# A hybrid decoder step on one core: half of down's token sums made in down, one accumulator bank for four products of the up quarters, operands asked for ahead, norms spread, the end by blocks

## The chip, the cores and the metric

The kernel runs on one core of one Trainium2 chip. The metric is the device time of one execution in microseconds. A core has five engines that run their own instruction streams beside each other: TensorE (PE: matrix products, with its weight loads shown as PEld), VectorE (DVE), ScalarE (ACT), GpSimd (POOL) and SyncE (SP, which here only issues DMAs). Products accumulate in eight PSUM banks; operands lie in SBUF; DMAs move data between SBUF and device memory.

## The reference, cut to what matters

One decoder layer for 2048 prompt tokens and 64 sample tokens (8 sequences of 8), width 1024: a mixer (DeltaNet heads and windowed attention), an output projection, then a gated ConvFFN with 2 x 2816 hidden columns, and a last RMSNorm. The change lies almost wholly in the FFN and the last norm:

```python
h = _rmsnorm(x, norm_ffn_w[i]) * (1 + sc2) + sh2
u = jnp.einsum('bld,df->blf', h, ffn_w_up[i])               # up
u_c, n_f_buf = _causal_dwconv(u, f_buf, ffn_conv_w[i])      # width 3
gate, up = jnp.split(u_c + ffn_conv_b[i], 2, axis=-1)
x = x + g2 * jnp.einsum('blf,fd->bld', jax.nn.silu(gate) * up, ffn_w_down[i])   # down
...
y = _rmsnorm(x, final_norm_w)
```

## The kernel before, in words

**Layout.** Tokens run along the free dimension, channels along the 128 partitions. Every fp32 product is made of three passes: each operand is split into a high part (rounded, `...h`) and a low part (the rest, `...l`), and PE forms high x high, low x high and high x low. So each operand that comes from memory costs an ACT cast (the high part) and a DVE or POOL subtraction (the low part).

**Stages.** adaLN and the input projection (0 to about 760 us of the span), mixer, output projection, `up_proj` for the first half of the tokens and a few channel blocks of the second, then the *up quarters* (about 1830 to 2280), then *down* (to the end).

**Beside the first stages** `weight_sums` (L1547) makes sums of down's weight blocks (`ws_d`): it loads two blocks into `suv` (L1553), takes four DVE sums (L1556 to L1559) and stores them (L1562). Its loads stand in SP's queue among those of the adaLN weights (`wada`) and the input projection (`w_raw`). The adaLN result is copied by ACT (`ms`, L184) and transposed by PE (`adat_ps`, L188).

**The up quarters** (`up_quarters`, `Quarters`) form, for the second half of the tokens (1088 of them: 384 + 384 + 320), two channel blocks per step p (a gate block and an up block) by the seven-product scheme for 2 x 2 blocks (products of sums). The weights of step p come in two 512-KB loads, `rawu` and `rawg`; POOL makes the sums S1, S2 (L1353, L1354) and S3, S4 (L1356, L1357); each of the eight operands of a step is then split by ACT (`rh`, L1360) and DVE or POOL (`rl`, L1361) into a ring of six. `prods` (L1426) says which operand goes into which bank: `a`, `b`, `c` for the 384-token products, `u` and `g` for the 320-token ones. After each product `evac` (L1450) brings a bank out: before the change bank `a` is copied to `t1` by ACT (L1455), bank `b` is added to `t1` by DVE (L1457, L1462, L1466), each time before `b` is used again. `elementwise` (L1471) then does the convolution (ACT: Identity, L1437; DVE: taps, L1435), the gate (ACT Tanh, L1479; DVE, L1481) and the product with the up half (L1488), whose result `actq` is stored to `act_d`.

**Token sums.** down uses the seven-product scheme too, with the hidden channels in two halves, K1 and K2, of 11 blocks, and the tokens in two halves. So it needs, beside the plain blocks B.., four sums over tokens: T1 to T4. Before the change all four are made in the quarters: `diff_loads` (L1387) reads the first half's results back, into `d12` and `d22`, and `diffs` (L1397) makes, for each p of K1, three DVE subtractions (T3, T1, T2) with a store each, and for each p of K2 one or two (T4). SP issues all this in order: a load into `d12` or `d22` waits until the store from that buffer has landed, and the next weight load stands behind it.

**down** (`down_phase`, L1577) runs over two parts of the tokens (`ip`), and in each over the seven entries of `DOWN` (L1568: weight operand, token operand, token group, whether new accumulators start, where the result goes). An entry has 11 steps i; each loads a weight tile (`wr`, 128 x 512) and a token tile (`tr`, 128 x 512 or 576), splits both (L1599 ACT, L1600 DVE; six buffers of each), and issues 24 matmuls (`products`, L1641). The last three steps are done accumulator by accumulator, so that the residual (`residual`, L1184) and the sums of squares for the last norm can start. The norm (`norm`, L1604) takes the sums over channels on PE (`ss_ps`), the root on DVE and POOL, brings it to all partitions by PE (`rb_ps`) and ACT (`drB`), and multiplies: four tiles on DVE (L1617), four on POOL (L1615). It is a generator; it is advanced between the products of the next entry, which starts with only six of its eight accumulators while a norm is pending (`free`). At the very end the last 576 tokens are done as blocks of 320 and 256 in the order of the last three steps only; both norms come after the last products.

**What sets the order.** Each engine runs its instructions in the order in which this code issues them, sorted by the tile framework; waits come from buffers and banks that are used again.

Of the kernel before, what the change touches and what calls it, by code (L numbers as in the profile page):

```python
# [94 lines left out]
def kernel(  # L95
# [22 lines left out]
    ts_d = {t: scratch(f"{t}_d", [KH, P, n]) for t, n in (("T1", LH), ("T2", LT - LH), ("T3", LH), ("T4", LT - LH))}  # L118
# [233 lines left out]
    def rest(steps):  # L352
        for _ in steps:
            pass
# [854 lines left out]
    def up_proj(hf, h, uc, op, ms=range(MU)):  # L1209
# [3 lines left out]
        def evac(m, bi, ps):  # L1213
# [7 lines left out]
            if m % 2 == 0:  # L1221
                silu2(cv, rb)
            else:
                nc.vector.tensor_tensor(cv, cv, sg[bi], ALU.mult)
                nc.sync.dma_start(act_d[m // 2, :, c0:c0 + n], cv)
# [146 lines left out]
    def up_quarters(first, q, h, W, uc, us, pq, sums_done):  # L1372
# [14 lines left out]
        def diff_loads(p):  # L1387
            if p in K1:
                for t, k in ((d12, p), (d22, K2[K1.index(p)])):
                    nc.sync.dma_start(t[:, :LH], act_d[k, :, :LH])  # L1390
                return
            i = K2.index(p)
            nc.sync.dma_start(d22, ts_d["T2"][i])
            if i + 8 < KH:
                nc.sync.dma_start(d12, ts_d["T2"][i + 8])

        def diffs(p):  # L1397
            sub = lambda out, a, b: nc.vector.tensor_tensor(out, a, b, ALU.subtract)
            if p in K1:
                i = K1.index(p)  # L1400
                sub(sg[:, :LH], d22[:, :LH], d12[:, :LH])
# [11 lines left out]
            if i + 8 < KH:  # L1413
                nc.sync.dma_start(sg, act_d[K2[i + 8], :, c0:])
            sub(d22, act, d22)
            nc.sync.dma_start(ts_d["T4"][i], d22)
            yield
            yield
            if i + 8 < KH:
                sub(d12, sg, d12)  # L1420
                nc.sync.dma_start(ts_d["T4"][i + 8], d12)
# [4 lines left out]
        prods = [[("B11", "a"), ("X1", "u")], [("T2", "b")], [("B21", "a"), ("X2", "u")], [("T3", "b")], [("X1", "g")],  # L1426
# [23 lines left out]
        def evac(j, bk, ru, rg):  # L1450
# [3 lines left out]
            if j == 0:  # L1454
                copy(t1, ps("a"))  # L1455
            elif j == 1:
                tt(U2, ps("b"), t1, ALU.add)  # L1457
            elif j == 2:
                copy(ru[:, cols[0]], ps("a"))
                copy(ru[:, cols[2]], bk["u"][:, :n - 2 * nx])  # L1460
            elif j == 3:
# [536 lines left out]
```

## Time and profile before

| | us |
|---|---|
| median of 3 runs | 2795.57 (2795.16 to 2802.66) |
| profiled execution, whole | 2792.84 |
| its span | 2791.1 |
| outside its span | 1.74 |

The profile's busy shares of the span are 95% for PE, 69% for DVE, 46% for ACT and 29% for POOL; the mean granted clock of TensorE is 0.979 of full.

By stage, of the same profiled execution:

| stage, us of the span | PE busy | DVE | ACT | POOL | clock | GB/s |
|---|---|---|---|---|---|---|
| 0 to 760 | 707.80 | 541.72 | 355.47 | 241.34 | 0.98 | 159 |
| quarters, 1830 to 2254 | 404.75 | 338.74 | 188.22 | 236.93 | 0.98 | 166 |
| end of the quarters, down, 2254 to 2791 | 497.60 | 323.19 | 227.20 | 70.04 | 0.96 | 192 |

In the views of the trace a group's row has line, engine, operation, output <- inputs (buffer numbers left out), shape, count, then busy time, mean duration in ns, and the idle time of the engine just before with what ended it. A waits row has engine, tile, line, what it waited for, then total us, times, longest. A windows row has the stretch, its length, busy time and count of PE, PEld, DVE, ACT and POOL, the granted clock, the busy share of the DMA engines and GB/s. A timeline row has start, duration and instruction, in brackets the idle time before it and its releaser.

### The profile page before, as it was taken

The numbers are of one execution on the slowest core, as the hardware profiler recorded it, in microseconds if no ns is written. First come the engines' busy times: TensorE is split into PE (matmuls) and PEld (weight loads), VectorE is DVE, ScalarE is ACT, GpSimd is POOL, SyncE is SP. The second block draws the span as 40 slices with busy tenths as digits, with TensorE's granted clock in tenths as the row PEclk, the third lists the DMA queues.
The fourth block names the chain that finished last, engine by engine and source line by source line (L and its number), as shares of the span: only waits on it lengthen the run. The fifth ranks groups of instructions, "written<-read, shape, count | busy, mean of one in ns | idle before, by whom it ended". The sixth has DMA issues, their size and how long they took to land.

```text
span 2791.1 us, 52033 instructions
## 1 busy us (share of the span) xinstructions
PE 2651.8 (95%) x19394; PEld 2480.7 (89%) x19394; DVE 1923.3 (69%) x3947; ACT 1270.9 (46%) x3327; POOL 822.6 (29%) x711
## 2 busy tenths in 40 slices
PE   7899999999999899999999999899999989999997
PEld 6788987788999898888888999899989989999997
DVE  6666479898413887888777646888877765665655
ACT  5444265554322654554544534554334444443443
POOL 2015243442313422222131114246555600121021
PEclk9999999999999999999999999999999999999998
DMA  7874443332445443332264445134455557565644
GB/s 278 297 269 143 127 135 108 90 98 78 133 122 187 141 118 87 96 95 74 72 215 134 142 144 190 64 118 169 156 182 187 171 177 246 178 205 193 223 154 138
DMA packets 311177, 428.21 MB, mean 153 GB/s; under 512 B 82275, under 2 KB 217924, under 8 KB 310660
## 3 DMA queue, kind: packets, MB, share of 16 engines
q1 hardware_dynamic: 310924, 424.89, 47.0%
q8 instruction: 152, 2.49, 0.4%
q14 instruction: 101, 0.83, 0.1%
HBM read 304.71 MB, written 121.09 MB: 153 GB/s over the span
## 4 chain that ended last, share of the span: by engine, by line
PE 69%; DVE 15%; DMA 6%; ACT 3%; issue 3%; POOL 2%; SPq 1%; DVEq 0%; ACTq 0%; POOLq 0%
PE up_ps L323 18%; PE dn_ps L1641 15%; PE in_ps L323 12%; PE op_ps L323 6%; DVE ev L522 2%; PE uq_b L1510 2%; DMA T_d<-d 2%; DMA rawg<-in_w_upT_dram 1%; PE uq_c L1510 1%; PE as_ps L917 1%; PE pv_ps L954 1%; PE uq_a L1510 1%; PE uq_g L1510 1%; PE uq_u L1510 1%; DVE gt L699 1%
## 5 line engine op out<-in xcount | busy, mean ns | idle before, releaser
L323 PE MATMUL up_ps<-hi,w_hi 128*128 128x384 f32 (+2 forms) x1152 | 379.5, 329 | 8.7 <-ACT cv L517 7.9
L323 PE MATMUL up_ps<-hi,w_lo 128*128 128x384 f32 (+2 forms) x1152 | 373.9, 325 | 1.0 <-DVE w_lo L315 1.0
L323 PE MATMUL up_ps<-lo,w_hi 128*128 128x384 f32 (+2 forms) x1152 | 371.6, 323 | 0.0
L1641 PE MATMUL dn_ps<-tl,wh 128*128 128x256 f32 (+1 forms) x1232 | 354.5, 290 | 14.2 <-DVE tl L1600 14.2
L1641 PE MATMUL dn_ps<-th,wl 128*128 128x256 f32 (+1 forms) x1232 | 353.3, 290 | 0.0
L323 PE MATMUL in_ps<-hi,w_hi 128*128 128x384 f32 (+2 forms) x1056 | 347.1, 333 | 6.2 <-DVE ev L572 2.6
L323 PE MATMUL in_ps<-lo,w_hi 128*128 128x384 f32 (+2 forms) x1056 | 348.5, 330 | 2.2 <-DVE lo L265 1.3
L323 PE MATMUL in_ps<-hi,w_lo 128*128 128x384 f32 (+2 forms) x1056 | 346.2, 328 | 0.5 <-POOL w_lo L315 0.5
L1641 PE MATMUL dn_ps<-th,wh 128*128 128x256 f32 (+1 forms) x1232 | 337.2, 289 | 8.5 <-DVE actq L1488 7.6
L1641 PEld LDWEIGHTS dn_ps<-tl,wh 128*128 128x128 f32 x1232 | 239.6, 194 | 15.3 <-DVE tl L1600 15.3
L323 PEld LDWEIGHTS up_ps<-hi,w_hi 128*128 128x128 f32 x1152 | 219.2, 190 | 30.5 <-issue 15.9
L1641 PEld LDWEIGHTS dn_ps<-th,wl 128*128 128x128 f32 x1232 | 239.3, 194 | 0.0
L1641 PEld LDWEIGHTS dn_ps<-th,wh 128*128 128x128 f32 x1232 | 230.2, 192 | 9.3 <-issue 7.8
L323 PEld LDWEIGHTS up_ps<-hi,w_lo 128*128 128x128 f32 x1152 | 218.8, 190 | 9.3 <-issue 7.0
L323 PEld LDWEIGHTS up_ps<-lo,w_hi 128*128 128x128 f32 x1152 | 219.0, 190 | 7.1 <-issue 6.2
L323 PEld LDWEIGHTS in_ps<-hi,w_hi 128*128 128x128 f32 x1056 | 200.1, 191 | 19.6 <-issue 10.3
L323 PEld LDWEIGHTS in_ps<-lo,w_hi 128*128 128x128 f32 x1056 | 201.3, 191 | 14.9 <-issue 9.5
L323 PEld LDWEIGHTS in_ps<-hi,w_lo 128*128 128x128 f32 x1056 | 201.4, 191 | 5.9 <-issue 4.4
L314 ACT CAST w_hi<-w_raw 128x1024 fp32r<-128x1024 f32 x124 | 129.6, 1046 | 120.8 <-PE op_ps L323 48.4
L1600 DVE TENSOR_TENSOR wl<-wr,wh 128x512 fp32r<-128x512 f32 x154 | 110.6, 718 | 106.7 <-ACT wh L1599 106.6
L315 DVE TENSOR_TENSOR w_lo<-w_raw,w_hi 128x1024 fp32r<-128x1024 f32 x95 | 119.1, 1254 | 91.5 <-ACT w_hi L314 89.1
L522 DVE SCALAR_TENSOR_TENSOR ev<-rb,cw,ev 128x384 f32<-128x384 f32 (+1 forms) x216 | 149.8, 698 | 42.8 <-ACT ev L515 40.5
(478 smaller groups left out, 6664.0 us busy)
## 6 DMA issues: line engine op xcount, KB each, us to landing
w_raw<-in_w_upT_dram SPq DMA_DIRECT2D x50, 512.0 KB
wada<-in_w_ada_dram SPq DMA_DIRECT2D x44, 512.0 KB
w_raw<-in_w_inT_dram SPq DMA_DIRECT2D x44, 512.0 KB
wr<-ws_d SPq DMA_DIRECT2D x88, 256.0 KB
proj<-ev SPq DMA_DIRECT2D x88, 192.0 KB
wr<-in_w_downT_dram SPq DMA_DIRECT2D x66, 256.0 KB
tr<-T_d SPq DMA_DIRECT2D x66, 256.0 KB
w_raw<-in_w_outT_dram SPq DMA_DIRECT2D x32, 512.0 KB
```

Source lines behind the costliest of these rows:

```text
L314: nc.scalar.copy(hi, raw)
L315: (eng or nc.vector).tensor_tensor(lo, raw, hi.bitcast(F32), ALU.subtract)
L323: nc.tensor.matmul(ps[:, :n], a[:, k, :], b[:, k, :n], start=first is not False and k == ks[0] and i == 0, stop=last is not False and k == ...
L522: nc.vector.scalar_tensor_tensor(out, src(j), w[:, j:j + 1], out, ALU.mult, ALU.add)
L699: nc.vector.tensor_tensor(tv, G[:np_, j, j + 1:].unsqueeze(2).broadcast_to(shape), T0[:, j, 0:j + 1].unsqueeze(1).broadcast_to(shape), ALU ...
L917: nc.tensor.matmul(banks[v][:, 256 * g + P * k0:256 * g + 256], qs[r, g0 + g], kw[r, P * k0:], start=True, stop=True, tile_position=(64 * ...
L954: nc.tensor.matmul(pv_ps[64 * v:64 * v + 64, :], (vprev[0], vt)[half][:, 64 * v:64 * v + 64], PT[v, half], start=half == k0, stop=half == 1)
L1510: nc.tensor.matmul(bk[t][:, :nb], u[:, k], v[:, k], start=new and k == 0 and y == 0, stop=k == KG - 1 and y == 2, skip_group_check=True)
L1600: nc.vector.tensor_tensor(l, raw, h.bitcast(F32), ALU.subtract)
L1641: nc.tensor.matmul(acc[m, s][:, :width[s]], w[i][a][:, c], t[i][b][:, r], start=new and i == 0 and y == 0, stop=i == KH - 1 and y == 2, sk ...
```

## The change

1. **Early loads.** `weight_sums` asks for its two blocks only behind the last weight load that was issued (`tc.issue_after(loads[-1])`).
2. **Silu.** `up_proj` for the second half of the tokens and the quarters use ACT's Silu in place of Tanh and a DVE instruction; the factor 2 that the rest of the code carries goes into the multiplication with the up half (a TENSOR_TENSOR becomes a SCALAR_TENSOR_TENSOR).
3. **One bank for four products.** In the quarters B11, T2, T3 and T4 of the up scheme now add up in bank `b` without a restart; ACT copies the running sum out after each (`t1`, U2, U3, then the gate block). The three DVE adds onto `t1` are gone; a DVE add for B21 (bank `a` plus `t1`) takes the place of an ACT copy.
4. **Token sums.** In the quarters a K1 step makes only T3 and T1 (T1 now 1088 tokens wide, one store), a K2 step only E, the difference of its own two halves. T2 = B22 - T1 and T4 = T1 + E are made in down, from two loads (`tr` and a new `tx`, two buffers) and one DVE instruction per step.
5. **Operands ahead.** down asks for the operands of step i + 3 ahead of the products of step i, across entries too (`ahead`, `AHEAD` = 3).
6. **Norms spread.** The norm's parts are advanced behind the first steps (i = 1 and 3) of the next entry's first pass, not after it.
7. **The end by blocks.** The last entry runs all 11 steps for its block of 320 tokens, then all 11 for the block of 256; the weights of steps 6 to 10 stay in buffers of their own, the first block's norm runs beside the second block's products, and the last sum of squares is kept apart (`dsl`).
8. **Banks at down's start.** The list of banks is permuted for the first entry (`banks[:1] + banks[4:] + banks[1:4]`).

```diff
-        prods = [[("B11", "a"), ("X1", "u")], [("T2", "b")], [("B21", "a"), ("X2", "u")], [("T3", "b")], [("X1", "g")],
+        prods = [[("B11", "b"), ("X1", "u")], [("T2", "b")], [("B21", "a"), ("X2", "u")], [("T3", "b")], [("X1", "g")],
                  [("T1", "c")], [("T4", "b"), ("X2", "g")], [("B22", "c")]]
...
-            if j == 0:
-                copy(t1, ps("a"))
-            elif j == 1:
-                tt(U2, ps("b"), t1, ALU.add)
+            if j in (0, 1, 3):
+                copy((t1, U2, None, U3)[j], ps("b"))
             elif j == 2:
-                copy(ru[:, cols[0]], ps("a"))
+                tt(ru[:, cols[0]], ps("a"), t1, ALU.add)
...
-            nc.scalar.activation(rg[:, :n], dg, AF.Tanh, scale=0.5)
+            nc.scalar.activation(sg, dg, AF.Silu)
             yield
-            nc.vector.scalar_tensor_tensor(sg, rg[:, :n], 1.0, dg, ALU.add, ALU.mult)
...
-                sub(d12[:, :LH], d12[:, :LH], act[:, :LH])
-                nc.sync.dma_start(ts_d["T1"][i], d12[:, :LH])
                 yield
-                sub(d22[:, :LH], d22[:, :LH], d12[:, :LH])
-                nc.scalar.copy(d22[:, LH:], act[:, LH:])
-                nc.sync.dma_start(ts_d["T2"][i], d22)
+                sub(d12, d12, act)
+                nc.scalar.mul(d12[:, LH:], act[:, LH:], -1.0)
+                nc.sync.dma_start(ts_d["T1"][i], d12)
...
             for x, k in enumerate((K1[i], K2[i])):
-                nc.sync.dma_start(uv[:, x], I["w_downT"][k])
+                with tc.issue_after(loads[-1]):
+                    nc.sync.dma_start(uv[:, x], I["w_downT"][k])
...
+            if name == "T2":
+                raw, more = get("tr", "T1", r, RAWS), get("tx", "B22", slice(r.start, min(r.stop, PW)), 2)
+                c = more.shape[1]
+                nc.vector.tensor_tensor(raw[:, :c], more, raw[:, :c], ALU.subtract)
...
+            elif name == "T4":
+                raw, more = get("tr", "T1", r, RAWS), get("tx", "E", r, 2)
+                nc.vector.tensor_tensor(raw, raw, more, ALU.add)
...
+                for i in range(lead):
+                    ahead(f + min(i + AHEAD, DR - 1))
+                    products(i, head)
+                    if finish and i in (1, 3):
+                        next(finish)
...
+            if last:
+                for s in (1, 0):
+                    f = place[q, 0, subs[s].start]
+                    for i in range(KH - SIDE):
+                        ahead(f + i + AHEAD)
+                        products(i, [(m, s) for m in range(NM)])
+                        if finish and i:
+                            next(finish, None)
```

**How the rows move.** In SP's queue in the early stage, before the change, the first `suv` loads of the weight sums stand ahead of the projection's stores and loads:

```order
L479 DMA tu_s<-zero 64x512 [waits DMAHW5_49]
L1553 DMA suv<-in_w_downT_dram 128x1024 [waits DMAHW6_49]
L1553 DMA suv<-in_w_downT_dram 128x1024 [waits DMAHW7_49]
L578 DMA proj<-ev 128x384 [waits DMAHW0_49,DVE_49]
L306 DMA w_raw<-in_w_inT_dram 128x1024 [waits DMAHW1_49,Pool_49]
```

After the change, in SP's queue, they stand here:

```order
L168 DMA wada<-in_w_ada_dram 128x1024 [waits DMAHW7_49,PE_49]
L578 DMA proj<-ev 128x384 [waits DVE_49]
L306 DMA w_raw<-in_w_inT_dram 128x1024 [waits Pool_49]
L1547 DMA suv<-in_w_downT_dram 128x1024 [waits DMAHW2_49]
L1547 DMA suv<-in_w_downT_dram 128x1024 [waits DMAHW3_49]
L578 DMA proj<-ev 128x256 [waits DMAHW4_49,DVE_49]
```

They moved from the queue's positions 45 and 46 to 97 and 98, that is behind 52 other DMAs, and their DVE sums with them.

On ACT, inside one K1 step of the quarters, before the change (`rh` the casts of operands, `t` the copy of bank a, `rbg` the gate block, S the weight sums that POOL makes):

```order
L1360 CAST rh<-S_20422 128x512 [waits PE_49]
L1455 COPY t_21095<-uq_a 128x384 [waits PE_49]
L1360 CAST rh<-rawg 128x512 [waits PE_49]
L1479 ACTIVATE rbg_21092<-cq 128x1088 [waits DVE_49,Activation_49]
L1360 CAST rh<-S_21099 128x512 [waits PE_49,Pool_49]
L1459 COPY rbu_21090<-uq_a 128x384 [waits PE_49]
L1437 ACTIVATE cq<-rbu_21091,vcb,vcw 128x1088 [waits DVE_49]
```

After the change ACT has these rows at the same place of a step, up to the fourth copy of bank b (t, U, U, rbg):

```order
L1453 COPY t_21085<-uq_b 128x384 [waits PE_49]
L1363 CAST rh<-rawu 128x512 [waits DVE_49,PE_49]
...
L1473 ACTIVATE sgq<-cq 128x1088 [waits DMAHW4_49,DVE_49,Activation_49]
L1435 ACTIVATE cq<-rbu_21080,vcb,vcw 128x1088 [waits Activation_49]
L1363 CAST rh<-S_21089 128x512 [waits PE_49,Pool_49]
L1453 COPY U_21086<-uq_b 128x384 [waits PE_49]
...
L1363 CAST rh<-S_20421 128x512 [waits PE_49,Pool_49]
L1453 COPY U_21087<-uq_b 128x384 [waits PE_49]
...
L1460 COPY rbg_21082<-uq_b 128x384 [waits PE_49]
```

Bank b is now copied out four times per step by ACT, each copy behind a cast or an activation; two of the casts ahead of them wait for POOL.

On PE, where down's first norm falls between the products of the next entry, before the change (buffer numbers kept; `ss_ps` the sums of squares, `rb_ps` the root brought to all partitions, the last row the first product whose operand DVE makes behind the norm's multiplications):

```order
L214 MATMUL ss_ps_27245<-ones_82,dsum2_26565 128x1 [waits Pool_49]
...
L1641 MATMUL dn_ps_27084<-tl_27306,wh_27299 128x256 [waits DVE_49]
...
L222 MATMUL rb_ps_27259<-dg_27254,ones_82 128x128 [waits DVE_49]
L1641 MATMUL dn_ps_27265<-th_27098,wh_27092 128x256 [waits PE_49]
...
L222 MATMUL rb_ps_27259<-dg_27254,ones_82 128x128 [waits DVE_49] x3
L1641 MATMUL dn_ps_27266<-th_27098,wh_27092 128x256 [waits Activation_49]
...
L1641 MATMUL dn_ps_27084<-tl_27345,wh_27338 128x256 [waits DVE_49]
```

After the change PE has this there:

```order
L214 MATMUL ss_ps_27181<-ones_81,dsum2_26591 128x1 [waits DVE_49,Pool_49]
...
L1690 MATMUL dn_ps_27110<-tl_27125,wh_27118 128x256 [waits DVE_49]
...
L1690 MATMUL dn_ps_27110<-tl_27155,wh_27148 128x256 [waits DVE_49]
...
L222 MATMUL rb_ps_27243<-dg_27190,ones_81 128x128 [waits DVE_49] x4
...
L1690 MATMUL dn_ps_27267<-th_26978,wh_26972 128x256 [waits PE_49]
...
L1690 MATMUL dn_ps_27110<-tl_27308,wh_27301 128x256 [waits DVE_49]
```

Between the last `rb_ps` row and that product stand 28 matmuls before the change and 66 after it. DVE's own order there is the same in both: root, four `dg`, four multiplications, then the low parts of the next step.

At down's start the accumulators of both programs take the banks in one order (0, 7, 6, 5, 4, then 3, 2, 1): the permuted list does not show in the program as it is built.

More of the change, by code (lines that the diff above doesn't have):

```diff
@@ L1465, in evac @@
             elif j == 6:
-                tt(rg[:, cols[0]], ps("b"), t1, ALU.add)
+                copy(rg[:, cols[0]], ps("b"))
                 copy(rg[:, cols[2]], bk["g"][:, :n - 2 * nx])
@@ new lines, in down_phase, with ahead @@
+        blocks_of = lambda q, g: [slice(0, SW), slice(SW, wide(q, g))]
+        queue = [(q, i, slice(0, wide(q, DOWN[q % ND][2]))) for q in range(Q - 1) for i in range(KH)]
+        queue += [(Q - 1, i, blocks_of(Q - 1, 1)[s]) for s in (1, 0) for i in range(KH)]
+        place = {(q, i, r.start): f for f, (q, i, r) in enumerate(queue)}
+        done = [0]
+        def ahead(f):
+            while done[0] <= min(f, len(queue) - 1):
+                q, i, r = queue[done[0]]
+                get_w(q, i)
+                get_t(q, i, r)
+                done[0] += 1
@@ L1688, in down_phase @@
         rest(finish)
     BANKS = {"acc": 2, "fr": 2, "st": 1, "sc": 1, "at": 2}
[L1692 removed]
+    LEAD, SIDE, DR, RAWS, AHEAD, FREE = 5, 3, 6, 3, 3, 6
     CV = 5
```

287 lines of the change are left out of this document (162 added, 125 removed).

## Prediction

> **What bounds the kernel now.** I read the page first: PE is busy for 95% of the span and carries most of the chain that ended last. So a gain can come only from time in which PE waits or runs at a low clock, and from the tail behind its last product.
>
> ```profile
> PE 2651.8 (95%) x19394; PEld 2480.7 (89%) x19394; DVE 1923.3 (69%) x3947; ACT 1270.9 (46%) x3327; POOL 822.6 (29%) x711
> PE 69%; DVE 15%; DMA 6%; ACT 3%; issue 3%; POOL 2%; SPq 1%; DVEq 0%; ACTq 0%; POOLq 0%
> ```
>
> I then asked for PE's waits, stage by stage. Rows are: who waits, for whom, total us, times, longest. First the early stage, then the quarters, then down:
>
> ```profile
> PE adat_ps L188 <- ACT ms L184: 9.9, 1, 9.9
> PE uq_b L1510 <- DVE U L1457: 10.6, 6, 3.8
> PE uq_b L1510 <- POOL rl L1361: 5.6, 5, 1.8
> PE dn_ps L1641 <- DVE tl L1600: 14.2, 5, 4.8
> PE dn_ps L1641 <- DVE actq L1488: 7.6, 1, 7.6
> ```
>
> The reader sees five places, 47.9 us in all, and the change touches each of them. What follows a wait shows in the windows, which give the granted clock. All sums below are made against the profiled execution, 2792.84 us; the median of the runs stands 2.7 us above it (2795.57), and I add that at the end.
>
> **Early loads.** Who holds ACT's copy `ms` up is seen in the timelines of DVE and ACT:
>
> ```profile
> 93.66 0.69 DVE L1556 TENSOR_TENSOR suv<-suv 128x512 f32<-128x512 f32 x1 [4.19 <-DMA suv<-in_w_downT_dram]
> 96.05 0.52 ACT L536 ACTIVATE rb<-ev 128x384 f32<-128x384 f32 x1 [6.10 <-DVE ev L522]
> 60.00:100.00 40.00, 28.52 (x221) 26.14 (x222) 33.25 (x59) 21.79 (x65) 8.50 (x7) 0.92 0.54 184
> 100.00:140.00 40.00, 40.00 (x363) 33.03 (x363) 23.21 (x41) 17.22 (x46) 2.36 (x1) 0.91 0.99 372
> ```
>
> DVE sits 4.19 us in front of a weight sum whose operand has not landed, and everything behind it on DVE, then on ACT, then on PE, waits too. Four sums at 0.69 us stand among the taps: 4.19 + 4 x 0.69 = 6.9 us of the 9.9. The change moves these loads and sums behind 52 DMAs of SP's queue, so these 6.9 us go; late next are the `wada` loads themselves, since the DMA engines are 0.99 busy in the second window, so I keep the other 3.0 us. The window behind the gap has the clock at 0.91: 40 x 0.09 = 3.6 us of lost work. I take half of it back. Term: **-8.7** (bounds 0, if the weight loads set the pace anyway, and -13.5). "TensorE: Matmul & The Clock Gate" of the Trainium skill (section on the HAM clock gate) has half the clock until about 3.4 us have been busy again, which makes 1.7 us per gap and an early term of -7.8; the row has twice that.
>
> **The quarters.** The windows show where they are slow:
>
> ```profile
> 1880.00:1930.00 50.00, 48.99 (x298) 48.73 (x298) 41.92 (x47) 23.78 (x50) 29.31 (x25) 1.00 0.49 168
> 1930.00:1980.00 50.00, 44.50 (x259) 42.91 (x258) 38.95 (x44) 20.11 (x44) 28.25 (x24) 0.97 0.49 171
> 1980.00:2030.00 50.00, 46.17 (x264) 45.64 (x263) 40.56 (x45) 19.99 (x44) 28.78 (x24) 0.94 0.47 164
> 2030.00:2080.00 50.00, 47.56 (x270) 46.69 (x269) 38.25 (x45) 20.69 (x46) 28.09 (x24) 0.95 0.50 172
> 2080.00:2130.00 50.00, 46.19 (x265) 44.78 (x264) 39.50 (x45) 20.40 (x45) 27.94 (x24) 0.97 0.50 173
> 2130.00:2180.00 50.00, 49.91 (x302) 49.36 (x301) 40.18 (x49) 21.33 (x45) 26.17 (x25) 1.00 0.61 204
> ```
>
> A step has 132 matmuls (84 of 384 columns, 48 of 320). At the best rate, 302 per 50 us, it takes 21.9 us; in the four slow windows (K1 steps) 259 + 264 + 270 + 265 = 1058 matmuls take 200 us, which is 8 steps of 25.0. So 24.8 us is all that these windows can give; the windows with 298 and others near it add 3.8. Something longer than PE's own work goes round once a step; POOL, ACT and SP say what:
>
> ```profile
> POOL S L1353 <- DMA rawg<-in_w_upT_dram: 93.3, 17, 9.5
> ACT rh L1360 <- POOL S L1354: 109.4, 15, 10.2
> SPq L1390 <- DMA T_d<-d: 56.1, 20, 5.9
> L1398 DVE TENSOR_TENSOR d<-d,actq 128x1024 f32<-128x1024 f32 x11 | 21.8, 1986 | 0.2
> L1398 DVE TENSOR_TENSOR d<-d,d 128x1024 f32<-128x1024 f32 x11 | 20.4, 1859 | 0.1
> L1481 DVE SCALAR_TENSOR_TENSOR sgq<-rbg,cq 128x1088 f32<-128x1088 f32 x17 | 21.9, 1287 | 17.1 <-ACT rbg L1479 9.4 <-DMA T_d<-sgq 6.5 <-ACT rh L1360 1.2
> L1457 DVE TENSOR_TENSOR U<-uq_b,t 128x384 f32<-128x384 f32 x18 | 9.9, 551 | 1.2 <-PE uq_b L1510 1.2
> L1455 ACT COPY t<-uq_a 128x384 f32<-128x384 f32 x18 | 8.5, 472 | 3.1 <-PE uq_a L1510 3.0
> L1356 POOL TENSOR_TENSOR S<-rawu,rawg 128x512 f32<-128x512 f32 x17 | 32.5, 1910 | 0.0
> L1353 POOL TENSOR_TENSOR S<-rawg 128x512 f32<-128x512 f32 x17 | 24.0, 1412 | 93.3 <-DMA rawg<-in_w_upT_dram 93.3
> L1435 DVE SCALAR_TENSOR_TENSOR cq<-rbg,vcw,cq 128x1024 f32<-128x1024 f32 x36 | 46.0, 1278 | 5.2 <-ACT cq L1437 5.2
> ```
>
> The round is: `rawg` lands, POOL sums, ACT and POOL split, SP may issue; but in SP's queue the reloads of `d12` and `d22` stand ahead of the next `rawg`, each behind the landing of the store from that buffer, and that store behind DVE's chain T1, then T2. The change takes one link out: the subtraction for T2 (1.86 us) with its 544-KB store; T1's store now stands where T2's stood, so the last reload still waits for one. I count only the DVE link: 8 steps x 1.86 = **-14.9**. Beside this, DVE loses 1.29 (L1481) and three adds of 0.55 and gains one, ACT gains three copies of about 0.47 and loses one: both keep room (DVE is busy 0.8 of these windows, ACT 0.4), so I cost this at nothing, and the 10.6 us of waits for U are in the 24.8. Bounds: 0 (the new round is no shorter) and -28.6 (all slow windows at 302). "GPSIMD Engine Reference" of the Trainium skill (section Key points) lets POOL contend with DVE instructions of two SBUF inputs; one such instruction fewer per step would by that page bring the three POOL sums from 1.91 us (L1356) nearer to 1.41 (L1353) and shorten the round further; the rows agree only in part (L1398 takes 1.99 us, L1435 with as many inputs and columns 1.28), and I take no credit for it.
>
> At the end of the quarters PE waits 7.6 us for the last `actq`. One DVE instruction of 1.29 us leaves that chain, and the permuted banks change nothing, as the order of the built program shows: **-1.3** (bounds 0 and -2.6, two chains).
>
> **The norms.**
>
> ```profile
> 2461.26 6.92 DVE L1617 SCALAR_TENSOR_TENSOR x<-x,nw,drB 128x512 f32<-128x512 f32 x4 [3.49 <-ACT drB L223]
> 2340.00:2380.00 40.00, 40.00 (x336) 40.00 (x335) 24.57 (x47) 13.89 (x25) 0.00 (x0) 1.00 0.55 179
> 2440.00:2480.00 40.00, 34.77 (x279) 34.36 (x278) 22.10 (x32) 12.90 (x25) 11.61 (x11) 0.96 0.46 153
> 2520.00:2560.00 40.00, 35.51 (x252) 35.08 (x251) 18.56 (x28) 10.83 (x18) 8.29 (x6) 0.91 0.52 179
> 2700.00:2740.00 40.00, 35.51 (x253) 35.07 (x253) 24.79 (x39) 15.23 (x26) 8.12 (x6) 0.96 0.50 171
> ```
>
> Four multiplications hold DVE for 6.92 us, and the low parts of the next step stand behind them. DVE's order is the same after the change; what moves is PE: 66 instead of 28 matmuls stand between the norm's last row and the product that needs those parts. A matmul of 256 columns takes 40 / 336 = 0.119 us, so 38 x 0.119 = 4.5 us of cover are added to each of three norms whose waits are 4.8 at most: 13.5 of the 14.2 us go. The clock in the three windows lost 1.6 + 3.6 + 1.6 = 6.8 us; gap and aftermath lie in the same windows, so half, 3.4, counts. Term: **-16.9** (bounds -8, if the rows for the sums now wait, and -21).
>
> **The end.**
>
> ```profile
> 2770.30 0.48 DVE L1184 SCALAR_TENSOR_TENSOR x<-dn_ps,MOD,x 128x256 f32<-128x256 f32 x1 [0.59 <-PE dn_ps L1641]
> 2774.23 4.30 DVE L1617 SCALAR_TENSOR_TENSOR x<-x,nw,drB 128x320 f32<-128x320 f32 x5 [0.32 <-ACT drB L223]
> 2778.45 0.41 DVE L1196 TENSOR_TENSOR dsum<-dsum,sq 128x256 f32<-128x256 f32 x1
> L1195 ACT ACTIVATE sq<-x 128x256 f32<-128x256 f32 x49 | 20.2, 415 | 17.2 <-DVE x L1184 12.8 <-DVE dsum L1196 3.6 <-POOL dsum L1196 0.5
> ```
>
> After the last product both norms follow one another, and the second's sum (done at 2778.86) stands behind the first's multiplications. With the first norm beside the second block's products the sum is ready at 2770.30 + 0.48 + 0.42, about 2771.2: 7.7 us less. I give 1.7 back for the first block's `rb_ps`, now inside the products. Term: **-6.0** (bounds -2 and -8).
>
> **What is added in down.** 44 more loads: 22 of 256 KB for T2 and 22 of 256 to 288 KB for T4, about 12 MB, and 44 DVE instructions of about 0.7 us (31 us).
>
> ```profile
> L1600 DVE TENSOR_TENSOR wl<-wr,wh 128x512 fp32r<-128x512 f32 x154 | 110.6, 718 | 106.7 <-ACT wh L1599 106.6
> 2254.00:2791.00 537.00, 497.60 (x3896) 495.04 (x3894) 323.19 (x541) 227.20 (x411) 70.04 (x75) 0.96 0.58 192
> ```
>
> DVE is free for 537 - 323 = 214 us here. In a T2 step 768 KB must come in 24 x 0.119 = 2.86 us, 275 GB/s, where a window above moved 372. So PE's work hides both; but `tx` has two buffers, and T4 in the last entry has steps of half the length. If that cover is gone in the 22 T4 steps by 0.5 us and the T2 steps by as much, it costs 22. I take **+5** for it and the first steps (bounds 0 and 22). Silu in `up_proj`, the operands asked for ahead elsewhere, and the extra switch of ACT's table lie beside PE's work in windows with PE at 40.00 of 40: nothing.
>
> **Sum.** -8.7 - 14.9 - 1.3 - 16.9 - 6.0 + 5 = -42.8: 2750.0 for the profiled execution, 2752.7 for the median, rounded to 2753.
>
> **The rivals.**
>
> *The round in the quarters is not shorter.* For it: the last reload still waits for a store, and rawu's load is still behind POOL's split. Against it: one store and one subtraction fewer. Then the 14.9 us stay: 2768.
>
> *down becomes bound by its token operands.* For it: three loads and three DVE instructions a step where there were two and two. Against it: 372 GB/s and 214 free us. Price 22 in place of 5: 2770.
>
> *The spread norms wait in another place.* The sums of squares stand earlier on PE, so PE may wait for POOL's last addition instead. Then some 9 of the 16.9 stay: 2762.
>
> *Slower: the chain through bank b.* Four products in a row use one bank, each behind ACT's copy of the last, and ACT's copies stand behind casts that wait for POOL's sums (the order of ACT). With nothing else in the way a copy is hidden by the product between. If each of the four is late by y, a step takes 21.9 + 4y, and 18 steps cost 72y over the floor, which is 2753 - 13.7 = 2739. Slower than 2804 it is from y = 0.9 us on; at 1.0 it gives 2811. For it: ACT waits 109.4 us for POOL's sums today. Against it: most of that wait is for `rawg`'s load, with PE's work queued before it.
>
> **How the numbers follow.** My forecast gets 0.55, the first rival 0.17, down's operands 0.10, the spread norms 0.10, the bank chain 0.08 (of which 0.06 beyond the point). A measurement of this kernel can tell about 0.3%, 8.4 us, from no change; faster than 2787 is then 0.86, within it 0.08 (two rivals together), slower 0.06. The range goes from 2735 (the quarters at -28.6 and the early loads at -13.5) to 2785 (two rivals together).
>
> **What would show it.** Right: `adat_ps` waits under 4 us; the four windows of the quarters hold over 280 matmuls; the waits for `tl` in down are below 3 us in all; about 13 us from the last product to the span's end. Wrong: a new wait of PE on ACT's U or rbg copies in the quarters (the bank chain), on `tr` or `tx` behind DMA in down, or of `ss_ps` on POOL.

## The result and the profile after

| | before | after | ratio after / before |
|---|---|---|---|
| median | 2795.53 us (4 runs, 2795.16 to 2802.66) | 2755.72 us (4 runs, 2747.36 to 2759.84) | 0.9848 (95%: 0.9819 to 0.9877) |
| profiled execution, span | 2791.1 | 2745.6 | |

The change makes the kernel 39.8 us faster by the medians; 2753 was forecast. The profiled execution of the changed kernel is the fastest of its four; a second one (run e1 below) has a span of 2758.1. The first lines of the page after:

```profile
span 2745.6 us, 52204 instructions
PE 2638.5 (96%) x19404; PEld 2472.7 (90%) x19404; DVE 1891.1 (69%) x3936; ACT 1300.8 (47%) x3394; POOL 807.1 (29%) x711
PE 64%; DVE 19%; DMA 8%; issue 4%; ACT 3%; POOL 2%; SPq 0%; DVEq 0%; ACTq 0%; POOLq 0%
```

PE's waits in the changed kernel, first the early stage, then the end of the quarters and down:

```profile
PE rb_ps L222 <- DVE dg L218: 8.8, 3, 6.6
...
PE adat_ps L188 <- ACT ms L184: 1.6, 1, 1.6
...
PE dn_ps L1690 <- DVE actq L1481: 9.7, 1, 9.7
PE ss_ps L214 <- DVE dsum L1196: 4.7, 2, 3.2
PE dn_ps L1690 <- DVE tl L1601: 3.8, 7, 1.0
```

`adat_ps` fell from 9.9 to 1.6, `tl` from 14.2 to 3.8, and the waits of `uq_b` for U are gone. The wait for `actq` grew from 7.6 to 9.7. To see where the time came from, I read when each stage starts. These rows of a tile's view (duration min/median/max in ns, first and last start in us) are of before, then of after; the first row of each is the output projection, the others the first product kind of down:

```profile
L323 PE MATMUL op_ps<-mixh,w_hi x384: 278/337/632, 827.4 to 1743.2; 128*128 128x384 f32 x128, 128*128 128x256 f32 x32, 128*128 128x320 f32 x32
L1641 PE MATMUL dn_ps<-th,wh x1232: 274/283/551, 2275.7 to 2769.7; 128*128 128x256 f32 x152, 128*128 128x320 f32 x24
```

```profile
L323 PE MATMUL op_ps<-mixh,w_hi x384: 277/337/561, 818.7 to 1731.4; 128*128 128x384 f32 x128, 128*128 128x256 f32 x32, 128*128 128x320 f32 x32
L1690 PE MATMUL dn_ps<-th,wh x1192: 274/283/550, 2235.9 to 2719.8; 128*128 128x256 f32 x188, 128*128 128x320 f32 x11
```

With the first start of the quarters (1827.1 and 1815.3) and of the last product of down (2770.0 and 2729.4, where the last weights have tile names of their own) from the same traces, the stages read:

| stage | before | after | difference | e1 (after again) |
|---|---|---|---|---|
| up to the output projection | 827.4 | 818.7 | -8.7 | 823.4 |
| from there to the quarters | 999.7 | 996.6 | -3.1 | 1000.7 |
| quarters, to down's first product | 448.6 | 420.6 | -28.0 | 424.4 |
| down, first to last product | 494.3 | 493.5 | -0.8 | 493.6 |
| tail | 21.1 | 16.2 | -4.9 | 16.1 |
| sum | 2791.1 | 2745.6 | -45.5 | 2758.1 |

The quarters gave 24 to 28 us where 14.9 were forecast, down as a whole nothing. The windows of the quarters show the first:

```profile
1930.00:1980.00 50.00, 50.00 (x305) 50.00 (x304) 38.08 (x43) 27.82 (x56) 28.18 (x26) 1.00 0.55 175
1980.00:2030.00 50.00, 50.00 (x306) 49.71 (x304) 35.81 (x41) 26.38 (x53) 26.88 (x26) 1.00 0.51 170
2030.00:2080.00 50.00, 48.99 (x297) 48.67 (x296) 40.60 (x43) 26.94 (x58) 32.46 (x30) 1.00 0.47 161
2080.00:2130.00 50.00, 50.00 (x304) 50.00 (x303) 33.39 (x41) 27.86 (x55) 28.27 (x29) 1.00 0.64 210
```

Where 259 to 270 matmuls stood in 50 us there are 297 to 306, at full clock (284 to 306 in e1).

For down I split the 3696 products into its 14 entries of 264 and took the time from each entry's first product to the next one's (the 14th to the last product):

| entry | what is special | before | after | e1 (after again) |
|---|---|---|---|---|
| 1 | start, waits for actq | 41.4 | 44.3 | 44.4 |
| 2, 3 | T2 made; S3 behind it | 63.4 | 64.8 | 64.3 |
| 6, 8, 13 | a norm pending (8 also starts part two) | 127.8 | 111.2 | 111.3 |
| 7, 9 | T4 made; T2 made | 68.3 | 70.3 | 71.4 |
| 14 | T4 made; by blocks after | 35.1 | 44.5 | 43.8 |

The norms gave 16.6 us back as forecast; entry 14 took 9.4 of them away, the start and the other T entries 6.4.

### The profile page after: what moved, and what is told of

Same layout as the page of the kernel before. It is cut to its first block, busy times and chain, and to the rows that moved or that the text cites. A ratio compares the mean times of both kernels' runs of the same rounds, so it can differ in the third digit from the quotient of the medians.

```text
span 2745.6 us, 52204 instructions
## 1 busy us (share of the span) xinstructions
PE 2638.5 (96%) x19404; PEld 2472.7 (90%) x19404; DVE 1891.1 (69%) x3936; ACT 1300.8 (47%) x3394; POOL 807.1 (29%) x711
## 4 chain that ended last, share of the span: by engine, by line
PE 64%; DVE 19%; DMA 8%; issue 4%; ACT 3%; POOL 2%; SPq 0%; DVEq 0%; ACTq 0%; POOLq 0%
PE up_ps L323 16%; PE in_ps L323 12%; PE dn_ps L1690 10%; PE op_ps L323 6%; PE uq_b L1503 4%; DVE ev L522 3%; PE uq_c L1503 2%; PE uq_g L1503 2%; PE uq_u L1503 1%; DVE ht L258 1%; PE pv_ps L954 1%; PE as_ps L917 1%; DMA tr<-T_d 1%; DVE gt L699 1%; DMA tx<-act_d 1%
## 5 line engine op out<-in xcount | busy, mean ns | idle before, releaser
L1690 PE MATMUL dn_ps<-th,wh 128*128 128x256 f32 (+1 forms) x1192 | 333.2, 289 | 13.7 <-DVE actq L1481 9.7
L1690 PE MATMUL dn_ps<-tl,wh 128*128 128x256 f32 (+1 forms) x1192 | 340.6, 289 | 2.8 <-DVE tl L1601 2.8
L1690 PE MATMUL dn_ps<-th,wl 128*128 128x256 f32 (+1 forms) x1192 | 338.7, 288 | 0.0
L1690 PEld LDWEIGHTS dn_ps<-tl,wh 128*128 128x128 f32 x1192 | 229.6, 193 | 4.2 <-DVE tl L1601 4.1
L1690 PEld LDWEIGHTS dn_ps<-th,wl 128*128 128x128 f32 x1192 | 229.0, 193 | 0.0
```

What stands on the lines that cost most here:

```text
L1690: nc.tensor.matmul(acc[m, s][:, :n], w[q, i][a][:, c], th[b][:, v], start=new and i == 0 and y == 0, stop=i == KH - 1 and y == 2, skip_gro ...
```

## Theories

My theory behind the forecast was: in the quarters the round of reloads, stores and subtractions was longer than PE's work, so one subtraction less is what counts, and the one bank is free. The rival: the DVE adds between PE's products were the limit, so the one bank is what counts. For the end: the blocks save 6 us. The rival after the result: the blocks cost more than they save, or T4 made in down does. The runs below undo or do one part each. A run's own profile gives the stage times; 95% intervals are of the ratio to the kernel before on the same chip.

## Experiments

### e1: the changed kernel again

No edit.

> The changed kernel as it is, as the yardstick for the other runs of this call. Both theories: about 2755 us (2747 to 2760 so far). The spread of its own runs, 12 us, is far above that of the kernel before (8 us with one outlier); if it comes from the chip and not from the kernel, it should show in the other kernels of this call too.

Measured: 2754.73 us (2751.96 to 2759.91), 0.9847 (0.9820 to 0.9875). The kernel before, beside it, spread from 2791.0 to 2805.6. So the spread is not a matter of this kernel; both have it, and I judge single parts by stage times.

### e2, e3, e4: the two ends of down

e2 does the last entry in one pass again:

```diff
-                stay = q == Q - 1 and i >= DR
+                stay = False
...
-        queue = [(q, i, slice(0, wide(q, DOWN[q % ND][2]))) for q in range(Q - 1) for i in range(KH)]
-        queue += [(Q - 1, i, blocks_of(Q - 1, 1)[s]) for s in (1, 0) for i in range(KH)]
+        queue = [(q, i, slice(0, wide(q, DOWN[q % ND][2]))) for q in range(Q) for i in range(KH)]
...
-            order = [(m, s) for m in range(NM) for s in range(2)]
+            order = [(m, s) for s in (1, 0) for m in range(NM)] if last else [(m, s) for m in range(NM) for s in range(2)]
...
-            if last:
-                for s in (1, 0):
...
-                finish = norm(1, [(0, PW)], x, sums[1], cols[1])
+                finish = norm(1, [(SW, wide(q, 1) - SW), (0, SW)], x, sums[1], cols[1], True) if last else norm(1, [(0, PW)], x, sums[1], cols[1])
```

e3 makes the convolution's accumulator `cq` take banks 1 to 3 by touching it second:

```diff
         more = iter(())
+        for tag, name, w in (("b", "uq_b", 512), ("cq", "cq", 3 * 512)):
+            nc.vector.memset(pq.tile([P, w], F32, tag=tag, name=name, bufs=1)[:, :1], 0.0)
```

e4 has both.

> The last entry of down in one pass again over its 576 tokens, only the last three steps by blocks, both norms behind the last product; all else as after the change. Theory (the blocks cost more than they save: the tail is 4.9 us shorter but the entry 9.4 us longer): the last entry back to 35 to 37 us, the tail to about 21, in all 4 to 5 us faster than e1. Rival (the entry is long because T4 is now made in down, blocks or not): the entry stays at 41 to 44 us and the tail goes back to 21, so 2 to 5 us slower than e1.

Measured: 2750.57 us (2747.03 to 2754.66), 0.9831 (0.9803 to 0.9858). Entry 14 takes 35.5 us, the tail 18.9: together 54.4, against 59.9 in e1 and 56.2 before. The theory holds: as the change has it, the end by blocks is a loss of 5.5 us against one pass. By the medians e2 is 4.2 us ahead of e1, with ranges that overlap.

> The convolution's three banks of the quarters are placed on banks 1 to 3, so that the five accumulators with which down starts (banks 0, 7, 6, 5, 4) are none of them; all else as after the change. Theory (PE's wait of 9.7 us for the last actq is for the banks alone): the wait goes, the first entry of down takes about 33 us in place of 44, 8 to 11 us faster than e1. Rival (the operands of down's first products are late as well, behind the same store and its queue): another wait takes its place, less than 3 us faster.

Measured: 2748.18 us (2742.93 to 2750.37), 0.9819 (0.9792 to 0.9846). The first 40 us of down, in the change and then in e3:

```profile
2236.00:2276.00 40.00, 30.31 (x229) 30.13 (x230) 21.70 (x32) 12.21 (x21) 0.20 (x1) 0.83 0.60 205
```

```profile
2242.00:2282.00 40.00, 35.64 (x286) 35.07 (x287) 26.29 (x42) 15.76 (x28) 0.20 (x1) 0.99 0.76 261
```

The wait for `actq` falls from 9.7 to 1.0 us and the first entry from 44.4 to 33.0, but the second grows from 32.4 to 36.4; there PE now waits 2.7 us for DVE's residuals (`x`), 0.5 in e1. The theory holds with less than its price, 7.5 us of the two entries in place of 8 to 11; the medians are 6.6 us apart. What matters for the change: its permuted list of banks did nothing, while the order in which the tiles are first touched moved the wait.

> Both edits of e2 and e3 together. Theory: they are at opposite ends of down and add up: 12 to 16 us faster than e1, about 2741. Rivals: the sum of what the two rivals say, within 5 us of e1.

Measured: 2739.78 us (2738.27 to 2741.95), 0.979 (0.976 to 0.982). That is 15.0 us below e1, within the 12 to 16 expected; e2 and e3 alone were 4.2 and 6.6 us below it, so they add up and a little more, for which no run has a reason.

### e5, e10, e9, e6: the parts of the quarters

e5 puts `B11` into bank `a` again with the three DVE adds (the lines of the change's first hunk of `prods` and `evac` undone). e10 undoes Silu too. e9 is the kernel before with Silu alone. e6 is the changed kernel with the four token sums made in the quarters:

```diff
-            if name == "T2":
+            if name == "none2":
...
-            elif name == "T4":
+            elif name == "none4":
```

with `ts_d`, `diff_loads` and `diffs` as before the change.

> The four products in one bank undone in the quarters (bank a for B11, DVE adds onto t1 again); token sums, Silu and all else as after the change. The quarters took 448.6 us before and 420 to 424 after. Theory A (the round through the reloads behind the token sums' stores was the limit): they stay at 420 to 430 us, and the kernel within 6 us of the change. Rival B (the DVE adds between PE's products were the limit): they go back to 435 us or more, and waits of uq_b for U come back with over 5 us.

Measured: 2747.73 us (2742.87 to 2748.63), 0.9821 (0.9801 to 0.9840). Two of its eight windows, all alike:

```profile
1930.00:1980.00 50.00, 50.00 (x305) 50.00 (x304) 39.69 (x46) 25.14 (x52) 29.38 (x27) 1.00 0.54 173
2030.00:2080.00 50.00, 50.00 (x305) 50.00 (x304) 40.04 (x49) 24.27 (x53) 32.65 (x28) 1.00 0.50 161
```

The quarters take 417.5 us, with PE at 305 matmuls per 50 us from end to end. Rival B falls: without the one bank nothing comes back. The one bank even costs: 419 to 424 us in the quarters with it, 1 to 7 more, and the first entry of down 44.4 against 39.6, of which e5's next two entries give 1.9 back. The medians say 7.0 against e1 (on another chip), and 7.9 for e12 against e4 (also on another chip). PE's wait for the last `actq` is 6.3 us in e5 and 9.7 in e1; why `actq` comes later relative to PE with the one bank was not tried.

> The change without Silu and without the one bank: of its edits in the quarters only the token sums are left. Theory (one subtraction and one store less is enough, and with it the round is under PE's work): the quarters take 417 to 422 us, as without the one bank alone (417.5). Rival (Silu's DVE instruction is needed too): 425 to 435 us.

Measured: 2760.48 us (2755.51 to 2770.52), 0.9873 (0.9849 to 0.9898). Quarters 424.9 us, at the edge between theory and rival. Its slowest windows:

```profile
1980.00:2030.00 50.00, 49.19 (x298) 48.55 (x297) 36.18 (x46) 21.62 (x46) 27.32 (x25) 1.00 0.50 175
2030.00:2080.00 50.00, 46.59 (x278) 45.57 (x278) 38.05 (x45) 23.06 (x49) 27.77 (x25) 1.00 0.48 163
```

So the token sums alone are worth 448.6 - 424.9 = 23.7 us here, and leave 7 us, to e5's 417.5, that Silu removes. With Silu already there they are worth 436.3 (e9) - 417.5 (e5) = 18.8.

> The kernel before with Silu alone (in up_proj for the second half of the tokens and in the quarters): one DVE instruction of 1.29 us less per step. With the token sums undone the quarters took 441.8 us against 448.6 before, and Silu is the likeliest of what was left in. Theory: the round in the quarters has that instruction in it, the quarters take 438 to 444 us, the kernel 4 to 10 us faster than before. Rival (Silu lies beside the round; the 6.8 us are from the one bank or from noise): 447 us or more, less than 3 us faster.

Measured: 2784.07 us (2777.79 to 2789.59, 7 runs), 0.9951 (0.9934 to 0.9969), so 13.7 us faster. Quarters 436.3 us. The theory holds and is undersized: 12.3 us for one DVE instruction of 1.29 us in each of 18 steps, where 4 to 10 were expected. DVE also stood idle for 17.1 us in front of these instructions (L1481 in the prediction); how much of the 12.3 is the wait and how much the instruction was not separated.

> The token sums undone: T1, T2, T3 and T4 are all made in the quarters again, down loads T2 and T4 ready-made; one bank, Silu and all else as after the change. Theory A: the quarters go back to 436 to 448 us; in down the entries of T2 and T4 get 1 to 3 us shorter each, the last one too if T4 is what makes it long (then 36 to 38 us in place of 44). Rival B: the quarters stay below 430 us. In all theory A has 2760 to 2775, rival B 2745 to 2755.

Measured: 2761.40 us (2757.39 to 2772.89), 0.9887 (0.9854 to 0.9919). Quarters 441.8 us: theory A holds, and the price of the token sums in the presence of the rest is 18 to 23 us. In down the T entries fall back (entries 2 and 3 31.7 each, 7 31.7, 9 35.3), and entry 14, still by blocks, takes 37.5 us with a tail of 13.1: 50.6 together. That is 5.5 less than before the change, close to the 6.0 forecast for the blocks. So the blocks are good with a ready-made T4 (e6) and bad with one made on the spot (e1 against e2).

### e11: more landing buffers

```diff
-    LEAD, SIDE, DR, RAWS, AHEAD, FREE = 5, 3, 6, 3, 3, 6
+    LEAD, SIDE, DR, RAWS, AHEAD, FREE = 5, 3, 6, 5, 3, 6
...
-                raw, more = get("tr", "T1", r, RAWS), get("tx", "E", r, 2)
+                raw, more = get("tr", "T1", r, RAWS), get("tx", "E", r, 4)
```

(and four `tx` for T2.)

> The changed kernel with more landing buffers in down: five each for tr and wr in place of three, four for tx in place of two. Theory (the entries with T2 and T4, above all the last one with its half-length steps, wait for landing buffers: SP waits for DVE there): the last entry falls from 44 to 37 to 39 us, the other T2 and T4 entries to within 1 us of those with ready-made sums, in all 7 to 12 us faster than the change, 2743 to 2748. Rival (DVE's and ACT's own work of those steps is the limit, or the low clock after a gap): less than 3 us.

Measured: 2748.36 us (2742.64 to 2750.40), 0.9822 (0.9806 to 0.9839). Both were right in part. The T entries 2, 7 and 9 fall to 31.7, 31.7 and 35.2, as with ready-made sums, so there the landing buffers were what was waited for. Entry 14 stays at 43.0, so there they were not, though the tail falls to 13.7 us. At the start they bring nothing: down's first product comes 13.4 us after the quarters' last, and PE waits 13.1 of them for ACT's casts, whose loads are late; the first entry is then 10 us shorter than in e1, and the two together 1.8 us longer. That the larger buffers lie where the quarters' still were is likely and was not shown.

### e8: the norm's rows at their old place

```diff
                     products(i, head)
-                    if finish and i in (1, 3):
-                        next(finish)
+                if finish:
+                    next(finish)
+                    next(finish)
```

> The norm's first parts are advanced behind the first pass again, as before the change; operands ahead and all else as after. Theory (the place of the norm's rows on PE gives the cover): the three entries with a norm go back from 34.7, 38.9 and 37.6 us towards 40.5, 44.0 and 43.3, and the kernel is 12 to 17 us slower than the change. Rival (asking three steps ahead is what hides them): the entries stay within 2 us of the change.

Measured: 2772.59 us (2769.49 to 2776.03), 0.9913 (0.9893 to 0.9934). Entries 6, 8, 13: 40.5, 44.4, 44.0, together 17.6 us more than in e1, and the old wait is back. PE's waits of e8:

```profile
PE dn_ps L1690 <- DVE tl L1601: 16.8, 6, 4.8
```

So asking ahead alone hides nothing of the norms, and the place of PE's rows is needed for all of it. Whether the place would do without asking ahead was not tried.

### e7: the early loads alone

The kernel before with `with tc.issue_after(loads[-1]):` around the loads of `weight_sums`.

> The kernel before with one edit of the change alone: the loads of the weight sums are asked for behind the last weight load. Theory: the wait of adat_ps falls from 9.9 us to under 3, the output projection starts 7 to 10 us earlier, and the whole kernel is 7 to 10 us faster than before, 2786 to 2789. Rival: what is put off comes back later in the mixer (weight sums among its DVE work), less than 3 us faster.

Measured: 2790.78 us (2785.41 to 2796.93, 10 runs), 0.9977 (0.9965 to 0.9990): 6.4 us faster, from 2.8 to 9.8. The wait of `adat_ps` is 1.6 us. Compared product by product, e7's profile is 10.5 us ahead of before's at 180 us; 4.7 us of it are lost between 210 and 257, about the wait of `rb_ps`. The profiled execution, the slowest of the ten, loses the rest later and has its output projection 2.4 us after before's. In the eleven profiles of kernels that have this edit among others the output projection starts 2.9 to 8.7 us earlier than before. So a part comes back, as the rival had it, but not all.

### e12: what the runs point to

The change with the edits of e2, e3 and e5.

> The change with three edits: the last entry of down in one pass, the convolution's banks off down's first five, the one bank undone. Theory (they act at different places and add up): quarters 417 to 419 us with every window at 305 matmuls, first entry of down 33 us, last entry and tail 55 us together; 2731 to 2736. Rival: without the one bank the start of down waits elsewhere and the sum is not reached, 2738 to 2745.

Measured: 2731.89 us (2728.27 to 2734.89), 0.9766 (0.9751 to 0.9782): 23 us below e1 and 65 below before. Quarters 418.3 us, first entry 31.8, last entry and tail 53.6. PE's largest waits in it from 1800 us on:

```profile
PE dn_ps L1695 <- DVE tl L1607: 3.9, 5, 1.5
PE rb_ps L222 <- DVE dg L218: 2.2, 2, 1.6
```

## Why the prediction came out right, term by term

The total was right to 3 us of the median, and in part by luck: two errors cancel. In the profile after, the quarters gave 13.1 us more than their term, and down's start, its T entries, entry 14 and the tail together 13.1 us less than theirs. The signs that the prediction named came true for `adat_ps` (1.6 us) and for the windows of the quarters (297 matmuls and more). They failed for `tl` (3.8 us where less than 3 was asked) and for the tail (16.2 us where 13 was). Its signs of being wrong hardly showed: PE waited 0.5 us for POOL at `ss_ps`, and its list of waits has none for U, `tr` or `tx`.

| term | forecast | measured | by |
|---|---|---|---|
| early loads | -8.7 | -6.4 (-9.8 to -2.8) | e7's times |
| quarters, token sums | -14.9 | -18 to -24 | e5 against e9, e10, e6 |
| quarters, Silu | 0 | -7 to -12 | e5 against e10, e9 |
| quarters, one bank | 0 | +1 to +7 | stage times against e5 |
| quarters together | -14.9 | -24 to -30 | stage times of after, e1 to e4, e8 |
| last actq | -1.3 | +3.0 | entry 1 |
| norms | -16.9 | -17.6 | e8 |
| the end | -6.0 | -5.5 with T4 ready-made | e6 |
| added in down | +5 | about +5, and 9.3 in entry 14 and the tail | e1 against e6 |

Each stage time is one profile's; two profiles of the changed kernel differ by 3.8 us in the quarters and by 4.6 at the output projection.

**The early loads.** Mechanism and size were right at the wait that was priced: it fell to 1.6 us and the clock in the two windows is full again. What I left out comes next: about the wait for `dg`, which was there before (6.2 us, now 6.6), 3.4 us are lost again of the 12.4 by which the same products came earlier until then, and the clock from 220 to 260 us is lower than before. Two windows after, then the last one before and after:

```profile
60.00:100.00 40.00, 36.58 (x318) 32.34 (x319) 33.31 (x60) 25.86 (x78) 8.49 (x7) 1.00 0.51 178
100.00:140.00 40.00, 40.00 (x394) 34.46 (x394) 17.00 (x31) 17.31 (x44) 2.38 (x2) 1.00 0.81 278
...
220.00:260.00 40.00, 33.34 (x213) 32.71 (x212) 29.32 (x49) 19.72 (x55) 16.85 (x14) 0.91 0.35 107
...
220.00:260.00 40.00, 35.83 (x216) 35.46 (x217) 31.14 (x56) 15.72 (x41) 19.39 (x21) 0.87 0.74 257
```

**The quarters.** The step "I count only the DVE link: 8 steps x 1.86" was mis-sized, and "I cost this at nothing" was wrong for Silu (e9: -12.3 alone). That the adds were not the limit is shown: with the three of them back, e5 has the fastest quarters of all runs. That the token sums were is shown too (e6, e10). That they act through a round that brings the weights late is what the waits in the traces point to, in two forms. In the kernels with the old banks it is POOL that waits for `rawg`, before, in e9, in e10 and in e5, with quarters of 448.6, 436.3, 424.9 and 417.5 us:

```profile
POOL S L1353 <- DMA rawg<-in_w_upT_dram: 93.3, 17, 9.5
POOL S L1356 <- DMA rawg<-in_w_upT_dram: 86.5, 17, 9.3
POOL S L1353 <- DMA rawg<-in_w_upT_dram: 69.6, 17, 7.4
POOL S L1356 <- DMA rawg<-in_w_upT_dram: 28.2, 17, 2.9
```

In the kernels with the one bank POOL's wait is the same for slow and fast quarters (42.0 us in e6, 41.3 after), and it is ACT that waits for `rawu`, in e6 (441.8 us) and after (420.6):

```profile
ACT rh L1363 <- DMA rawu<-in_w_upT_dram: 53.1, 14, 6.8
ACT rh L1363 <- DMA rawu<-in_w_upT_dram: 19.5, 11, 2.9
```

Which link of the round the token sums make shorter, the subtraction, its store or the reload behind it, no run separates. The prediction counted the subtraction in the eight steps of the slow windows; the change takes it out of all eleven K1 steps (x11 in its row), and 11 x 1.86 us are 20.4.

POOL's sums got shorter as well. Before, then after, in the window from 1930 to 2130 us:

```profile
L1354 POOL TENSOR_TENSOR S<-S,rawu 128x512 f32<-128x512 f32 x8 | 18.2, 2273 | 0.0
L1356 POOL TENSOR_TENSOR S<-rawu,rawg 128x512 f32<-128x512 f32 x8 | 17.2, 2151 | 0.0
...
L1357 POOL TENSOR_TENSOR S<-S,rawu 128x512 f32<-128x512 f32 x9 | 11.7, 1300 | 0.0
L1359 POOL TENSOR_TENSOR S<-rawu,rawg 128x512 f32<-128x512 f32 x9 | 11.6, 1294 | 0.0
```

By themselves they do not make the quarters fast: in e6 they take 1.30 us too, and in e5, the fastest, 1.35 and 1.65. "GPSIMD Engine Reference" of the Trainium skill (section Key points) states contention of POOL with DVE instructions that have two SBUF inputs. The rows do not speak against it as the prediction thought: L1435 has one input fewer in SBUF than L1398, since its `cq` lies in PSUM, and it keeps its 1.28 us beside POOL. But the number of DVE's instructions does not set the sums: e9 and e6 both keep the three subtractions, and the sums take 2.16 us in e9 and 1.30 in e6. That it is which of them fall beside each other is likely and was not tested.

The bound taken from the windows was nearly right: -28.6 was forecast as the most, and 448.6 - 417.5 = 31.1 was reached in e5, as PE's best rate was 305 per 50 us, not 302.

**The last actq and the one bank.** "I cost this at nothing" failed for the bank too, the other way: the wait for the last `actq`, forecast to fall by 1.3 us, grew by 2.1. The slower rival named the bank chain; a loss is there in small, 1 to 7 us in the quarters and up to 4.8 at down's start, far from the 0.9 us per link from which it would have decided.

**The norms.** Right in mechanism and size: 38 more matmuls of cover, 17.6 us.

**The end, and T4.** Here the step "first norm beside the second block's products" failed for the kernel as it is, by a link that I had named only as a danger ("T4 in the last entry has steps of half the length") and priced inside +5. That price also counted too little: down makes 33 T4 additions and not 22, as the last entry makes one for each of its 22 half steps. Entry 14 of the changed kernel, its first 28 us and the rest, and the same entry in e6 with T4 ready-made:

```profile
2686.00:2714.00 28.00, 26.74 (x182) 24.99 (x180) 23.13 (x58) 12.92 (x30) 5.49 (x6) 1.00 0.63 186
2714.00:2730.00 16.00, 14.37 (x94) 14.19 (x94) 9.73 (x23) 3.64 (x9) 3.90 (x4) 0.79 0.21 67
```

```profile
2705.00:2743.00 38.00, 37.59 (x282) 36.98 (x281) 29.45 (x67) 19.30 (x45) 10.01 (x10) 1.00 0.40 125
```

DVE is busy for 23.1 of 28 us there. The sums, splits and residuals of two blocks stand in one queue, and the first norm's sums of squares wait for DVE (PE 1.4 us). The clock falls to 0.79, but this is not what makes the entry long: in e1 it stays full and the entry takes 43.8 us. The same two stretches of e1:

```profile
2698.00:2726.00 28.00, 26.82 (x183) 25.28 (x182) 24.60 (x60) 13.73 (x32) 6.09 (x6) 1.00 0.63 188
2726.00:2742.00 16.00, 12.55 (x105) 12.20 (x103) 9.71 (x23) 4.11 (x10) 3.90 (x4) 1.00 0.27 79
```

In the tail the first norm's multiplications end up in front of the last residuals. In the changed kernel's timeline of DVE:

```profile
2725.61 4.36 DVE L1662 SCALAR_TENSOR_TENSOR x<-x,nw,drB 128x320 f32<-128x320 f32 x5 [2.86 <-ACT drB L223]
2729.89 1.26 DVE L1184 SCALAR_TENSOR_TENSOR x<-dn_ps,MOD,x 128x256 f32<-128x256 f32 x3
```

PE's last product started at 2729.38; the residuals that belong to the second block's first accumulators start only at 2729.89, and PE then waits 3.2 us for `dsum`. So the tail is 16.2 us, not the 13.1 of e6. More landing buffers hardly change entry 14 (e11, 43.0); what in DVE's queue costs how much was not separated.

## What to carry to other kernels

When a stage runs slower than its busiest engine, find the round that sets it and count every instruction in it: here 1.29 us of DVE in 18 steps were worth 12 us, with the waits in front of them, more than a half-microsecond add that PE was seen to wait for 10.6 us in all. A wait named in a list of waits is where the delay arrives, not what causes it: the adds onto `t1` were named, and undoing their removal cost nothing. Work that moves from a stage with a full queue into one with room has to be checked at that stage's tightest place, not against its mean: T4 fits into down's idle DVE time on the whole and costs 9 us in its last, half-length steps.

## What the runs showed of the hardware that was not expected

In the changed kernel PE waits only 1.43 us in entry 14, and some products of one column stand behind the wait. Then the start-to-start time of products of 256 columns goes from 0.12 to 0.21 us and stays there for several us. PE's timeline in the changed kernel:

```profile
2713.58 0.28 PE L1690 MATMUL dn_ps<-tl,wh 128*128 128x256 f32 x1
2715.29 0.35 PE L214 MATMUL ss_ps<-ones,dsum 128*128 128x1 f32 x2 [1.43 <-DVE dsum L1196]
...
2717.07 0.56 PE L214 MATMUL ss_ps<-ones,dsl 128*128 128x1 f32 x2
...
2718.07 0.41 PE L1690 MATMUL dn_ps<-tl,wh 128*128 128x256 f32 x1
2718.29 0.41 PE L1690 MATMUL dn_ps<-th,wl 128*128 128x256 f32 x1
```

The same place in e1, with a longer wait, keeps 0.12 us:

```profile
2729.11 0.35 PE L214 MATMUL ss_ps<-ones,dsum 128*128 128x1 f32 x2 [1.90 <-DVE dsum L1196]
...
2731.48 0.28 PE L1690 MATMUL dn_ps<-tl,wh 128*128 128x256 f32 x1
2731.60 0.28 PE L1690 MATMUL dn_ps<-th,wl 128*128 128x256 f32 x1
```

"TensorE: Matmul & The Clock Gate" of the Trainium skill (section on why this matters for kernels) asks for no idle gap above some 3 us. In the changed kernel a gap of half that length was followed by the low rate, in e1 a longer one was not. So the length of the gap alone does not decide here; what part the narrow products have was not tested.
